# RMSNorms of a two-layer trunk cut into drawn pieces, with their sums of squares mostly on GpSimd

## The chip, the cores and the metric

The kernel runs on one core of a Trainium2 chip. The metric is device time of one execution in microseconds (us). The engines are named as in the profile: PE is TensorE's matmul row and PEld its weight loads, DVE is VectorE, ACT is ScalarE, POOL is GpSimd, SP the engine whose queue issues nearly all DMAs.

## The reference

1152 tokens (1024 latent, 128 context) of width 1024 pass two layers. Layer 0 mixes by attention and a state-space scan, and ends in an output projection `w_out`; layer 1 mixes by pooling windows of 2, 4, 8 and 16 tokens. Each layer then has an MLP of 4096 hidden units with a squared ReLU. Before each mixer, before each MLP and at the end stands an RMSNorm:

```python
def rmsnorm(x, g):
    xf = x.astype(jnp.float32)
    y = xf * lax.rsqrt(jnp.mean(xf * xf, axis=-1, keepdims=True) + EPS)
    return y.astype(x.dtype) * g

def modulate(h, shift, scale):
    return h * (1 + scale) + shift

def sq_relu_mlp(h, w1, w2):
    return jnp.square(jax.nn.relu(h @ w1)) @ w2
```

So every norm needs, for each token, the sum of 1024 squares and one reciprocal root. Five norms are computed; the change touches four of them: norm 1 (after the projection, for MLP 0), norm 2 (after MLP 0, for the pooling), norm 3 (after the pooling, for MLP 1) and the final one (after MLP 1).

## The kernel before, in words

Channels lie on the 128 partitions, tokens along the free dimension. The tokens are three blocks of 384 (NB = 3, BN = 384), the channels eight slices (KT = 8), so one block of the residual is `x[b]`, 128 x 8 x 384 in float32. Block 2 holds 256 latent and 128 context tokens, which have their own gains, so its instructions are often two (SEGS). Matmuls run on a high and a low part of each operand (`hi`, `lo`; three products for one), which is why a weight tile has names such as `wh` and `wl`.

Each norm of a block has four parts:

- **The split** (`gains`, line 303): for each slice ACT writes `hi` = x times gain and DVE writes `lo` = x times gain minus `hi`. Both are the tiles `blk`, of two pools with three buffers each.
- **The sum** (`norm_sums`, line 260): ACT squares slice 0 into the tile `s`, then each later slice into a tile `r` (two buffers), and DVE adds it: seven `TENSOR_TENSOR s<-s,r` for a block. Then one matmul with `selbc` spreads the mean over the partitions, into the PSUM tile `npb`.
- **The root** (`norm_root`, line 279): ACT's Ln and Exp, then four DVE instructions, into the tile `y`.
- The use of `y`: in an MLP it multiplies the first product (`r<-p,y`), in the pooling it is turned by a small matmul `py` into `yc`, at the end it scales the output. `npb` and `py` share one PSUM tag with two buffers.

The stages around the change:

- **Projection** (loop over `order`, lines 1375 to 1396): 24 products of 24 matmuls, the last six being slices 6 and 7 of block 0, then 1, then 2. DVE adds each product to `x[b]`, and meanwhile computes modulation vectors from `mod_v` (`mod_vec`, line 1299: two 128 x 1024 `mj` instructions per vector).
- **MLP** (`mlp`, line 1399): 16 passes over the hidden units; in each, for each block, two first products of 24 matmuls (`p1`, two PSUM buffers), ReLU and square into `ph`, `pl`, and then `second` (line 1404), eight products of 6 matmuls for the block before, each added to `x[b]` (`x<-p,modc,x`).
- **Pooling** (lines 1506 to 1580): ten windows of 128 tokens. `window_products(i+1)` is written before `window_means(i)`; its results `yt` get a shift added on POOL.
- **Final norm** (`final`, line 1583): for blocks 0 and 1 ACT applies the gain and POOL multiplies by `y`; for block 2 DVE does both in one instruction. Each slice is stored by a DMA.

Who draws what: `norm_block` (line 1340) writes a whole norm at once, `norm_pieces` (line 1350) is a generator that yields twice or more, with the whole sum as one piece. At the projection, blocks 0 and 1 use the generator and block 2 the block form; all is then exhausted ahead of MLP 0. After MLP 0 blocks 0 and 1 use the block form, block 2 the generator. In the pooling, blocks 0 and 1 of norm 3 start after windows 3 and 6, two pieces per window.

The order of text isn't the order of an engine's queue. A scheduler runs over all instructions with a cost model, takes among those it holds ready the one that stands first in the text, and fixes each engine's queue; buffers of a tag go in the order of text. At run time each queue is in order. All instructions are made by one wrapper, so nearly all rows say L86; they are told apart by their tiles.

Of the kernel before, what the change touches and what calls it, by code (L numbers as in the profile page):

```python
# [8 lines left out]
F32 = mybir.dt.float32  # L9
# [9 lines left out]
KT = 8  # L19
TL, TX = 1024, 128  # L20
NTOK = TL + TX
NB = 3
# [50 lines left out]
def build(nc, tc, a, o, probe=None):  # L73
# [46 lines left out]
    def tt(e, out, x, y, op):  # L120
        return e.tensor_tensor(out, x, y, op=op)
# [131 lines left out]
        s = modc[layer][:, (3 * half + 1) * 8:(3 * half + 2) * 8]  # L253
        stt(V, avec[i], s, 1.0, ng[:, i, :, None].to_broadcast([128, KT, 2]), ALU.add, ALU.mult)

    last_bc = [None]
    last_p2 = [None]
    last_ms = [None]

    def norm_sums(xb, sq, s4, done=False):  # L260

        if not done:
            A.activation(s4, xb[0], AF.Square)
            for k in range(1, KT):
                A.activation(sq(k), xb[k], AF.Square)
                tt(V, s4, s4, sq(k, True), ALU.add)
            pb = psn([128, BN], F32, "npb", bufs=GB[0], tag="g")
            last_bc[0] = T.matmul(pb, selbc, s4, start=True, stop=True)
            return pb
        ps = psn([128, BN], F32, "nps", bufs=GB[0], tag="g")  # L270
        for k in range(KT):
            g = k % 4
            T.matmul(ps[32 * g:32 * g + 32], ones32, sq(k, True), start=k < 4, stop=k >= 4, tile_position=(0, 32 * g))
        A.activation(s4, ps, AF.Copy)
        pb = psn([128, BN], F32, "npb", bufs=GB[0], tag="g")
        last_bc[0] = T.matmul(pb, selbc, s4, start=True, stop=True)
        return pb

    def norm_root(pb, y, u):
# [5 lines left out]
        V.tensor_scalar(u, u, -0.5, 1.5, op0=ALU.mult, op1=ALU.add)  # L285
        tt(V, y, y, u, ALU.mult)
        return y

    def sq_tile(more=False):
        last = []  # L290

        def sq(k, again=False):
            if not again:
                last[:] = [hid([128, BN], F32, ("ph", "pl")[k % 2]) if more else HP([128, BN], F32, "r", bufs=2)]
            return last[0]

        return sq

    def norm_stats(xb, more=False):
        pb = norm_sums(xb, sq_tile(more), HP([128, BN], F32, "s", bufs=2))  # L300
        return norm_root(pb, HP([128, BN], F32, "y", bufs=YB[0]), HP([128, BN], F32, "s", bufs=2))

    def gains(i, b, k0, xs, hi, lo):

# [72 lines left out]
                A.activation(sqs[b][:, k], xs[b][k], AF.Square)  # L377

    def sums(b):
        return norm_sums(xs[b], lambda k, again=False: sqs[b][:, k], scratch(), True)  # L380

    def root(b, pb):
        ys.append(norm_root(pb, H([128, BN], F32, f"y{b}"), scratch()))
# [953 lines left out]

    rr = [None] * NB

    def norm_block(i, b):  # L1340


        hi, lo = blk2()
        gains(i, b, 0, parts(x[b]), parts(hi), parts(lo))
        if b == 0:
            shift_columns(modc[i // 2][:, 24 * (i % 2):24 * (i % 2) + 8], hi, lo)
        rr[b] = norm_stats(parts(x[b]))
        return hi, lo

    def norm_pieces(i, b, out, first):  # L1350

        hi, lo = blk2()
        out.append((hi, lo))
        y = rr[b] = HP([128, BN], F32, "y", bufs=YB[0])

        def split_(k):
            gains(i, b, k, *(parts(t[:, k:k + 2]) for t in (x[b], hi, lo)))
            if b == 0 and k == KT - 2:
                shift_columns(modc[i // 2][:, 24 * (i % 2):24 * (i % 2) + 8], hi, lo)

        if first:
            for k in range(0, KT, 2):
                split_(k)
            yield
        pb = norm_sums(parts(x[b]), sq_tile(), HP([128, BN], F32, "s", bufs=2))
        yield
        norm_root(pb, y, HP([128, BN], F32, "s", bufs=2))
        if not first:
            for k in range(0, KT, 2):
                yield  # L1370
                split_(k)

    h1, nps = [], []
    wo = {}
    order = [(d, b) for d in range(6) for b in range(NB)] + [(d, b) for b in range(NB) for d in range(6, KT)]
    t0, t1 = MODV[0]
    for n, (d, b) in enumerate(order):
        if n == 3:
            kinds()
        for t in range(t0 + 4 * (n - 4) // 3, min(t0 + 4 * (n - 3) // 3, t1)) if n >= 4 else ():  # L1380
            mod_vec(0, t)
            if t == t1 - 1:
                mod_bias(0, t0, t1)
                scale_vec(1)
        for dd in range(d, min(d + 2, KT)):
            if dd not in wo:
                wo[dd] = weights(a["w_out"][dd], [128, KT, 128], nm="w2", nb=3, pool=W2)
        p = p2([128, BN])
        mm_cat(p, wo[d], b)
        add_to(b, d, p, modc[0][:, 16:24])  # L1390
        if d == KT - 1 and b < NB - 1:
            nps.append(norm_pieces(1, b, h1, GF[b]))
        elif d == KT - 1:
            h1.append(norm_block(1, b))
        if nps and next(nps[0], 0) == 0:
            nps.pop(0)


    def mlp(layer, h, after, extra=None):
        gate = modc[layer][:, 40:48]  # L1400
        prev = None
        y = list(rr)

        def second(w2, b, hd_):
            for d in range(KT):
                p = p2([128, BN])
                n = 0
                for j in range(2):
                    for wi, hi_ in ((0, 0), (0, 1), (1, 0)):
                        T.matmul(p, w2[j][wi][:, d], hd_[j][hi_], start=n == 0, stop=n == 5)  # L1410
                        n += 1
                add_to(b, d, p, gate)

        for c in range(NFF // 2):
            w1 = [weights(a["w1"][layer, 2 * c + j], [128, KT, 128]) for j in range(2)]
            w2 = []
            for j in range(2):
                raw = raw_tile([128, KT, 128])
                dma(raw, a["w2"][layer, 2 * c + j].rearrange("p (k m) -> p k m", k=KT))
                hi = W2([128, KT, 128], F32R, "w2h", bufs=3)  # L1420
                lo = W2([128, KT, 128], F32R, "w2l", bufs=3)
                A.activation(hi, raw, AF.Copy)
                tt(V, lo, raw, hi, ALU.subtract)
                w2.append((hi, lo))
            cf = []
            for b in range(NB):
                hh = []
                for j in range(2):
                    n = BX if b == 0 else BN
                    p = p1([128, BX])  # L1430
                    mm3(p[:, :n], w1[j], [parts(t[:, :, :n]) for t in h[b]], KT)
                    if b == 0:
                        cf.append(HP([128, 2], F32, "cf", bufs=6))
                        V.tensor_copy(cf[j], p[:, BN:BX])
                    r = HP([128, BN], F32, "r", bufs=2)
                    tt(V, r, p[:, :BN], y[b], ALU.mult)
                    for s0, s1, q in SEGS[b]:
                        A.activation(r[:, s0:s1], r[:, s0:s1], AF.Relu, bias=cf[j][:, q:q + 1])
                    ph = hid([128, BN], F32R, "ph")
                    A.activation(ph, r, AF.Square)  # L1440
                    s = HP([128, BN], F32, "s", bufs=2)
                    tt(V, s, r, r, ALU.mult)
                    pl = hid([128, BN], F32R, "pl")
                    tt(V, pl, s, ph, ALU.subtract)
                    hh.append((ph, pl))
                if extra is not None:
                    extra(c, b)
                if prev is not None:
                    second(*prev)
                    if c == NFF // 2 - 1 and b > 0:  # L1450
                        after(b - 1)
                prev = (w2, b, hh)
        second(*prev)
        after(NB - 1)

    hs = []

    def after_mlp0(b):
        if b == 0:
            scale_vec(2)  # L1460
            scale_vec(3)
            tt(V, gps, modc[1][:, 16:24], pscale[:, :, None].to_broadcast([128, KT, 2]), ALU.mult)
        if b < 2:
            hs.append(norm_block(2, b))
        else:
            nps.append(norm_pieces(2, 2, hs, True))
            next(nps[0])

    def mods_1(c, b):
        if c < 12:  # L1470
# [2 lines left out]
            if c == 11 and b == 2:  # L1473
                mod_bias(1, 0, 48)

    for g in nps:
        for _ in g:
            pass
    nps.clear()
    mlp(0, h1, after_mlp0, mods_1)  # L1480


# [23 lines left out]
    def window_products(i):  # L1506
        s0 = 112 * i if i < 9 else TL
        b, e = divmod(s0, BN)
        if i in (0, SH1):
            csh[i > 0] = shift_products(int(i > 0))  # L1510
        if e + 128 <= BN:
# [60 lines left out]
    for i in range(10):  # L1572
        if i < 9:
            ws.append(window_products(i + 1))
        window_means(i, ws[i])
        if i in (3, 6, 9):
            nps.append(norm_pieces(3, i // 3 - 1, h2, i == 9))
        for _ in range(NP if 0 < i < 9 else 20 if i else NQ):
            if nps and next(nps[0], 0) == 0:
                nps.pop(0)  # L1580


    def final(b):
        y = norm_stats(parts(x[b]), b > 0)
        for k in range(KT):
            xk = x[b][:, k]
            if k not in FP[b]:
# [1 line left out]
            else:  # L1589
                A.activation(xk, xk, AF.Copy, scale=ng[:, 4, k:k + 1])  # L1590
                tt(P, xk, xk, y, ALU.mult)
            dma(o["y"][b][:, k], xk)

    mlp(1, h2, final)
    tc_ln.__exit__(None, None, None)
    W2.close()
    WA[0].close()
# [135 lines left out]
```

## Time and profile before

| what | value |
|---|---|
| three runs | 2549.8, 2550.6, 2551.59 us (median 2550.6) |
| the profiled execution | 2552.76 us |
| its span in the trace | 2551.0 us |
| mean granted clock of TensorE | 0.969 of 2.4 GHz |
| PE, PEld, DVE busy | 94%, 90%, 70% of the span |
| ACT, POOL busy | 34%, 10% of the span |

Read it from the top: the run's time is 1.8 us over the span; PE is busy in all but some 150 us, part of which lies in the first 700 us, which the change leaves alone but for a reordered buffer. A busy PE can still be slow, when the granted clock is at the lower of its two levels (1.2 and 2.4 GHz; 0.5 and 1.0 in the profile). The later part is: projection up to about 797 us, MLP 0 to 1629, pooling to 1713, MLP 1 to 2528, and what follows.

### The profile page before, as it was taken

What the parts mean: (1) busy time and instruction counts of PE and PEld (TensorE: products, weight loads), DVE (VectorE), ACT (ScalarE), POOL (GpSimd) and SP (SyncE); (2) the same over time, 40 slices, a digit from 0 to 9 for tenths busy, and PEclk for the clock granted to TensorE, in tenths of its full rate; (3) what the DMA queues carried; (4) which work ended last, traced back from release to release, by engine and by line L of the source; (5) the groups of instructions that cost most, each with busy time, mean ns of one, the idle gap of its engine ahead of it and who ended that gap; (6) DMA issues with size and microseconds to landing.
All of it is one profiled execution on the core that took longest, in us unless ns stands there. A gap on an engine that the chain in (4) does not pass through costs nothing.

```text
span 2551.0 us, 36404 instructions
## 1 busy us (share of the span) xinstructions
PE 2399.8 (94%) x14070; PEld 2296.1 (90%) x14070; DVE 1792.0 (70%) x3583; ACT 877.2 (34%) x1663; POOL 267.0 (10%) x274
## 2 busy tenths in 40 slices
PE   7987898898997999999999999889999999999996
PEld 3876697787897999999999999879999999999996
DVE  7379865889788777767777655886565555555557
ACT  4453365777615221222222222562122222222214
POOL 5455612100000000000000000120000000000002
PEclk8998998999998999999999999989999999999998
DMA  6334688423353232322332110011111111111102
GB/s 244 82 104 126 192 200 229 105 57 81 129 191 108 67 91 68 98 75 75 91 91 79 50 34 25 1 50 50 42 50 34 50 34 50 34 50 42 42 9 74
DMA packets 106491, 210.86 MB, mean 83 GB/s; under 512 B 10576, under 2 KB 67664, under 8 KB 105936
## 3 DMA queue, kind: packets, MB, share of 16 engines
q1 hardware_dynamic: 104080, 203.01, 27.0%
q10 hardware_dynamic: 2240, 5.54, 0.6%
q8 instruction: 111, 1.82, 0.3%
q14 instruction: 60, 0.49, 0.1%
HBM read 176.95 MB, written 31.56 MB: 82 GB/s over the span
## 4 chain that ended last, share of the span: by engine, by line
PE 64%; DVE 11%; issue 5%; ACT 4%; DMA 4%; POOL 1%; SPq 0%; POOLq 0%; DVEq 0%; ACTq 0%
PE p L86 61%; DVE mj L86 2%; DVE blk L86 1%; DMA raw<-in_w_dram 1%; DVE sc L86 1%; DMA raw<-in_mod_v_dram 1%; PE SP L86 1%; DVE nm L86 1%; ACT e L86 1%; PE tp L86 1%; DVE x L86 1%; DVE s L86 1%; ACT blk L86 1%; DVE zz L86 1%; DVE w2l L86 1%
## 5 line engine op out<-in xcount | busy, mean ns | idle before, releaser
L86 PE MATMUL p<-blk,wh 128*128 128x384 f32 (+1 forms) x3072 | 794.2, 340 | 0.0
L86 DVE SCALAR_TENSOR_TENSOR x<-p,modc,x 128x384 f32<-128x384 f32 (+2 forms) x1056 | 513.6, 513 | 142.6 <-PE p L86 138.7
L86 PEld LDWEIGHTS p<-blk,wh 128*128 128x128 f32 x3072 | 561.5, 189 | 1.6 <-issue 1.2
L86 PE MATMUL p<-blk,wl 128*128 128x384 f32 (+1 forms) x1536 | 520.8, 339 | 0.0
L86 PE MATMUL p<-ph,w2h 128*128 128x384 f32 x1536 | 514.9, 335 | 3.7 <-DVE x L86 3.7
L86 PE MATMUL p<-pl,w2h 128*128 128x384 f32 x1536 | 513.9, 335 | 0.0
L86 PE MATMUL p<-ph,w2l 128*128 128x384 f32 x1536 | 513.6, 334 | 0.0
L86 ACT ACTIVATE r<-r,cf 128x384 f32<-128x384 f32 (+2 forms) x256 | 129.8, 531 | 691.6 <-DVE r L86 691.5
L86 PEld LDWEIGHTS p<-ph,w2h 128*128 128x128 f32 x1536 | 288.3, 188 | 6.2 <-DVE x L86 3.6
L86 PEld LDWEIGHTS p<-blk,wl 128*128 128x128 f32 x1536 | 289.5, 188 | 0.1
L86 PEld LDWEIGHTS p<-pl,w2h 128*128 128x128 f32 x1536 | 288.3, 188 | 0.3
L86 PEld LDWEIGHTS p<-ph,w2l 128*128 128x128 f32 x1536 | 288.3, 188 | 0.1
L86 DVE TENSOR_TENSOR r<-p,y 128x384 f32<-128x384 f32 x192 | 106.2, 554 | 188.9 <-PE p L86 188.7
L86 ACT ACTIVATE wh<-raw 128x1024 fp32r<-128x1024 f32 x80 | 84.7, 1060 | 349.7 <-PE p L86 312.1
L86 DVE SCALAR_TENSOR_TENSOR mj<-raw,cb 128x1024 f32<-128x1024 f32 x128 | 156.1, 1220 | 13.6 <-DMA raw<-in_mod_v_dram 12.6
L86 ACT ACTIVATE w2h<-raw 128x1024 fp32r<-128x1024 f32 x74 | 77.3, 1057 | 221.2 <-PE p L86 161.5
L86 PE MATMUL pmm<-lo,wh 128*128 128x384 f32 (+1 forms) x384 | 137.8, 359 | 7.8 <-DVE lo L86 7.5
L86 PE MATMUL pmm<-hi,wh 128*128 128x384 f32 (+1 forms) x384 | 141.0, 368 | 0.8 <-ACT wh L86 0.8
L86 PE MATMUL pmm<-hi,wl 128*128 128x384 f32 (+1 forms) x384 | 136.6, 356 | 1.2 <-DVE wl L86 1.2
L86 DVE TENSOR_TENSOR s<-r 128x384 f32<-128x384 f32 x192 | 106.5, 555 | 40.1 <-ACT r L86 40.0
L86 POOL TENSOR_TENSOR pl<-pl,mx 128x256 f32<-128x256 f32 x18 | 18.6, 1039 | 1024.1 <-ACT pl L86 1024.1
L86 DVE TENSOR_TENSOR wl<-raw,wh 128x1024 fp32r<-128x1024 f32 x76 | 98.7, 1300 | 22.1 <-ACT wh L86 21.8
(278 smaller groups left out, 3346.5 us busy)
## 6 DMA issues: line engine op xcount, KB each, us to landing
raw<-in_w_dram SPq DMA_DIRECT2D x128, 512.0 KB, 3.6
raw<-in_mod_v_dram SPq DMA_DIRECT2D x64, 512.0 KB, 3.6
raw<-in_mod_w_dram SPq DMA_DIRECT2D x25, 512.0 KB, 4.6
raw<-in_w_in_dram SPq DMA_DIRECT2D x16, 512.0 KB, 4.8
Kd<-kS SPq DMA_DIRECT2D x32, 176.0 KB, 4.8
qS<-zz SPq DMA_DIRECT2D x12, 384.0 KB, 2.7
Q<-qS SPq DMA_DIRECT2D x32, 144.0 KB, 4.7
x<-in_x_dram SPq DMA_DIRECT2D x3, 1536.0 KB, 7.3
```

The costliest lines, as they stand in the source:

```text
L86: ins = f(*args, **kw)
```

## The change

All norms of the four sites become generators in small pieces, and a list `nps` of them is drawn from by `pull`, one piece at a time, between the products of the projection, of the MLPs' `second` and first products, and of the pooling. `until` draws as far as a use needs. The sum is kept in `y` itself (before: `s`), and the adds go to an engine that is passed in: `P` (POOL) for norms 1 and 2 and for blocks 0 and 1 of norm 3, `V` (DVE) for block 2 of norm 3 and for the final norm. In the pooling four pieces are drawn per window in place of two. The norm of the last block after each MLP gets its pieces (`post`) directly behind each add of the last `second`.

```diff
+    def pull():
+        if nps and next(nps[0], 0) == 0:
+            nps.pop(0)
+    def until(what, i, b):
+        while (i, b) not in what:
+            pull()
+    def begin(g):
+        next(g)
+        nps.append(g)
+    def summer(b, acc, e):
+        def square(k):
+            if k == 0:
+                A.activation(acc, x[b][:, k], AF.Square)
+            else:
+                sq = HP([128, BN], F32, "r", bufs=2)
+                A.activation(sq, x[b][:, k], AF.Square)
+                tt(e, acc, acc, sq, ALU.add)
+        def means():
+            pb = psn([128, BN], F32, "npb", bufs=GB[0], tag="g")
+            T.matmul(pb, selbc, acc, start=True, stop=True)
+            return pb
...
+    def norm_gen(i, b, out, order, e):
         hi, lo = blk2()
         out.append((hi, lo))
         y = rr[b] = HP([128, BN], F32, "y", bufs=YB[0])
+        square, means = summer(b, y, e)
...
+        if order == "both":
+            for k in range(KT):
+                square(k)
+                if k % 2:
+                    split_(k - 1)
+                yield
+        if order == "split":
+            for k in range(0, KT, 2):
+                split_(k)
+                yield
+        if order != "both":
+            for k in range(0, KT, 2):
+                square(k)
+                square(k + 1)
+                yield
+        yield
+        pb = means()
+        yield
+        norm_root(pb, y, HP([128, BN], F32, "s", bufs=2))
+        rooted.add((i, b))
+        if order == "sums":
             for k in range(0, KT, 2):
                 yield
                 split_(k)
...
-        if d == KT - 1 and b < NB - 1:
-            nps.append(norm_pieces(1, b, h1, GF[b]))
-        elif d == KT - 1:
-            h1.append(norm_block(1, b))
-        if nps and next(nps[0], 0) == 0:
-            nps.pop(0)
+        if d == KT - 1:
+            begin(norm_gen(1, b, h1, "split", P))
+        else:
+            pull()
...
                 add_to(b, d, p, gate)
+                if post:
+                    next(post)
+                pull()
...
+                    if c == 0:
+                        until(halved, 2 * layer + 1, b)
                     p = p1([128, BX])
                     mm3(p[:, :n], w1[j], [parts(t[:, :, :n]) for t in h[b]], KT)
...
+                    if c == 0:
+                        until(rooted, 2 * layer + 1, b)
                     r = HP([128, BN], F32, "r", bufs=2)
...
-        second(*prev)
-        after(NB - 1)
+        last = after(NB - 1)
+        second(*prev, last)
+        nps.append(last)
...
         if b < 2:
-            hs.append(norm_block(2, b))
+            begin(norm_gen(2, b, hs, "split", P))
         else:
-            nps.append(norm_pieces(2, 2, hs, True))
-            next(nps[0])
+            return norm_gen(2, b, hs, "both", P)
...
-    for g in nps:
-        for _ in g:
-            pass
-    nps.clear()
     mlp(0, h1, after_mlp0, mods_1)
...
         if i in (3, 6, 9):
-            nps.append(norm_pieces(3, i // 3 - 1, h2, i == 9))
-        for _ in range(NP if 0 < i < 9 else 20 if i else NQ):
-            if nps and next(nps[0], 0) == 0:
-                nps.pop(0)
+            begin(norm_gen(3, i // 3 - 1, h2, "split" if i == 9 else "sums", V if i == 9 else P))
+        for _ in range(4 if i else 0):
+            pull()
...
+    def final_gen(b):
+        y = HP([128, BN], F32, "y", bufs=YB[0])
+        square, means = summer(b, y, V)
+        for k in range(KT):
+            square(k)
+            yield
+        yield
+        pb = means()
+        yield
+        norm_root(pb, y, HP([128, BN], F32, "s", bufs=2))
         for k in range(KT):
...
             dma(o["y"][b][:, k], xk)
+            yield
...
     mlp(1, h2, final)
+    while nps:
+        pull()
```

Nothing else of the arithmetic or of the DMAs changes: the same squares, 84 adds, 12 spreading matmuls and 24 stores are issued.

## Rows read from the trace of the kernel before

**Rows 1.** The page: span, and busy time of each engine.

```profile
span 2551.0 us, 36404 instructions
PE 2399.8 (94%) x14070; PEld 2296.1 (90%) x14070; DVE 1792.0 (70%) x3583; ACT 877.2 (34%) x1663; POOL 267.0 (10%) x274
```

**Rows 2.** Windows: stretch, its length, busy us of each engine, clock, DMA.

```profile
core 0: us, PE busy (x) PEld busy (x) DVE busy (x) ACT busy (x) POOL busy (x), PEclk, DMA share, GB/s
780.00:805.50 25.50, 24.32 (x137) 23.71 (x135) 25.24 (x57) 16.40 (x37) 0.00 (x0) 1.00 0.21 63
805.50:827.00 21.50, 8.21 (x29) 6.34 (x28) 18.09 (x36) 10.07 (x20) 0.00 (x0) 0.68 0.29 98
1596.00:1629.50 33.50, 31.97 (x181) 30.57 (x179) 30.49 (x66) 22.09 (x49) 0.00 (x0) 1.00 0.00 1
1629.50:1644.00 14.50, 8.33 (x44) 7.67 (x43) 14.48 (x38) 7.79 (x20) 3.91 (x1) 0.65 0.00 1
1671.80:1685.00 13.20, 8.64 (x34) 7.34 (x34) 11.92 (x27) 6.18 (x15) 3.41 (x4) 0.61 0.01 1
1696.30:1709.00 12.70, 7.91 (x31) 6.53 (x31) 11.00 (x25) 7.38 (x17) 3.07 (x3) 0.60 0.01 2
1721.60:1730.00 8.40, 3.82 (x12) 3.14 (x12) 6.77 (x13) 5.87 (x11) 0.00 (x0) 0.80 0.49 131
2528.20:2551.00 22.80, 1.65 (x2) 0.50 (x2) 16.21 (x25) 2.38 (x5) 9.99 (x8) 0.57 0.39 138
```

**Rows 3.** Timeline of PE: start, us, instruction, idle before and releaser.

```profile
786.68 0.91 PE L86 MATMUL npb<-s,selbc 128*128 128x384 f32 x2 [1.18 <-DVE s L86]
...
810.69 1.27 PE L86 MATMUL npb<-s,selbc 128*128 128x384 f32 x2 [4.89 <-DVE s L86]
820.35 1.65 PE L86 MATMUL npb<-s,selbc 128*128 128x384 f32 x2 [8.39 <-DVE s L86]
...
1639.10 0.58 PE L86 MATMUL p<-w2l,blk 128*128 128x256 f32 x1 [4.34 <-DVE w2l L86]
...
1675.75 1.65 PE L86 MATMUL npb<-s,selbc 128*128 128x384 f32 x2 [3.92 <-DVE s L86]
...
1726.26 1.65 PE L86 MATMUL npb<-s,selbc 128*128 128x384 f32 x2 [4.58 <-DVE s L86]
```

**Rows 4.** Groups of DVE's instructions from 780 to 822 us: count, busy, mean ns.

```profile
L86 DVE SCALAR_TENSOR_TENSOR blk<-x,avec,blk 128x384 fp32r<-128x384 f32 (+2 forms) x32 | 14.2, 514 | 0.0
L86 DVE SCALAR_TENSOR_TENSOR mj<-raw,cb 128x1024 f32<-128x1024 f32 x7 | 8.5, 1221 | 0.1
L86 DVE TENSOR_TENSOR s<-s,r 128x384 f32<-128x384 f32 x15 | 8.3, 554 | 0.7 <-ACT r L86 0.4
```

**Rows 5.** Timeline of ACT during the last-but-four product of the projection.

```profile
775.67 0.52 ACT L86 ACTIVATE r<-x 128x384 f32<-128x384 f32 x1 [1.96 <-DVE x L86]
```

**Rows 6.** Timeline of POOL from 2505 to 2545 us.

```profile
2508.38 9.06 POOL L86 TENSOR_TENSOR x<-x,y 128x384 f32<-128x384 f32 x8 [795.98 <-DVE y L86]
2530.22 9.99 POOL L86 TENSOR_TENSOR x<-x,y 128x384 f32<-128x384 f32 x8 [12.77 <-ACT ph L86]
```

**Rows 7.** Timeline of DVE from 2509 us to the end.

```profile
2513.26 0.61 DVE L86 SCALAR_TENSOR_TENSOR x<-p,modc,x 128x384 f32<-128x384 f32 x1
...
2530.84 1.23 DVE L86 TENSOR_TENSOR s<-s,ph 128x384 f32<-128x384 f32 x1
...
2537.24 1.16 DVE L86 TENSOR_TENSOR s<-s,pl 128x384 f32<-128x384 f32 x1
...
2543.68 4.32 DVE L86 SCALAR_TENSOR_TENSOR x<-x,pack,y 128x384 f32<-128x384 f32 x8
```

**Rows 8.** Timeline of DVE: first and last of seven sums, norm 3, block 0.

```profile
1669.32 0.55 DVE L86 TENSOR_TENSOR s<-s,r 128x384 f32<-128x384 f32 x1
...
1675.13 0.56 DVE L86 TENSOR_TENSOR s<-s,r 128x384 f32<-128x384 f32 x1
```

**Rows 9.** Timeline of PE: first matmuls of two successive windows' means.

```profile
1665.30 0.59 PE L86 MATMUL p<-mx,ph 128*128 128x112 f32 x4
...
1669.89 0.59 PE L86 MATMUL p<-mx,ph 128*128 128x112 f32 x4
```

More of the change, by code (lines that the diff above doesn't have):

```diff
@@ L254, in scale_vec, with norm_sums @@
         stt(V, avec[i], s, 1.0, ng[:, i, :, None].to_broadcast([128, KT, 2]), ALU.add, ALU.mult)
-    last_bc = [None]
     last_p2 = [None]
     last_ms = [None]
[L260 to L269, printed above, removed]
+    def norm_sums(sq):
         ps = psn([128, BN], F32, "nps", bufs=GB[0], tag="g")
@@ L272, in norm_sums @@
             g = k % 4
-            T.matmul(ps[32 * g:32 * g + 32], ones32, sq(k, True), start=k < 4, stop=k >= 4, tile_position=(0, 32 * g))
+            T.matmul(ps[32 * g:32 * g + 32], ones32, sq[:, k], start=k < 4, stop=k >= 4, tile_position=(0, 32 * g))
+        s4 = scratch()
         A.activation(s4, ps, AF.Copy)
         pb = psn([128, BN], F32, "npb", bufs=GB[0], tag="g")
-        last_bc[0] = T.matmul(pb, selbc, s4, start=True, stop=True)
+        T.matmul(pb, selbc, s4, start=True, stop=True)
         return pb
@@ L287, in norm_root @@
         return y
[L289 to L301, printed above, removed]
     def gains(i, b, k0, xs, hi, lo):
@@ L379, in sums @@
     def sums(b):
-        return norm_sums(xs[b], lambda k, again=False: sqs[b][:, k], scratch(), True)
+        return norm_sums(sqs[b])
     def root(b, pb):
@@ L1338, in build @@
     rr = [None] * NB
[L1340 to L1350, printed above, removed]
+    h1, nps, rooted, halved = [], [], set(), set()
+    def pull():
[19 more added lines that the diff above has]
+            return pb
+        return square, means
+    def norm_gen(i, b, out, order, e):
         hi, lo = blk2()
@@ L1359, in split_ @@
                 shift_columns(modc[i // 2][:, 24 * (i % 2):24 * (i % 2) + 8], hi, lo)
-        if first:
+            if k == KT - 2:
+                halved.add((i, b))
+        if order == "both":
[5 more added lines that the diff above has]
+        if order == "split":
             for k in range(0, KT, 2):
                 split_(k)
-            yield
-        pb = norm_sums(parts(x[b]), sq_tile(), HP([128, BN], F32, "s", bufs=2))
+                yield
[6 more added lines that the diff above has]
+        pb = means()
         yield
         norm_root(pb, y, HP([128, BN], F32, "s", bufs=2))
-        if not first:
+        rooted.add((i, b))
+        if order == "sums":
             for k in range(0, KT, 2):
@@ L1371, in norm_pieces @@
                 split_(k)
-    h1, nps = [], []
     wo = {}
@@ L1402, in mlp, with second @@
         y = list(rr)
-        def second(w2, b, hd_):
+        def second(w2, b, hd_, post=None):
             for d in range(KT):
@@ L1508, in window_products @@
         b, e = divmod(s0, BN)
+        until(rooted, 2, b)
+        if e + 128 > BN:
+            until(rooted, 2, b + 1)
         if i in (0, SH1):
@@ L1576, in build @@
         if i in (3, 6, 9):
-            nps.append(norm_pieces(3, i // 3 - 1, h2, i == 9))
-        for _ in range(NP if 0 < i < 9 else 20 if i else NQ):
-            if nps and next(nps[0], 0) == 0:
-                nps.pop(0)
-    def final(b):
-        y = norm_stats(parts(x[b]), b > 0)
+            begin(norm_gen(3, i // 3 - 1, h2, "split" if i == 9 else "sums", V if i == 9 else P))
[11 more added lines that the diff above has]
+        norm_root(pb, y, HP([128, BN], F32, "s", bufs=2))
         for k in range(KT):
@@ L1592, in final @@
             dma(o["y"][b][:, k], xk)
+            yield
+    def final(b):
+        if b < 2:
+            begin(final_gen(b))
+        else:
+            return final_gen(b)
     mlp(1, h2, final)
+    while nps:
+        pull()
     tc_ln.__exit__(None, None, None)
```

## The prediction

> **What bounds the kernel now.** Read the page's busy times first: PE has 2399.8 of 2551.0 us [rows 1], so a change that adds no speed to matmuls can win only where PE stands still or runs at the lower clock. The windows come next, to find those places in the part that the change touches [rows 2]; for each I count as lost its length less PE's busy time times the granted clock (an estimate, since busy matmuls overlap). Projection to MLP 0: 25.50 - 24.32 = 1.2, and 21.50 - 8.21 x 0.68 = 15.9, together 17.1 us. End of MLP 0 and first window: 33.50 - 31.97 = 1.5, and 14.50 - 8.33 x 0.65 = 9.1, together 10.6. Pooling, block 0 of norm 3: 13.20 - 8.64 x 0.61 = 7.9. Block 1: 12.70 - 7.91 x 0.60 = 8.0. Block 2, at the start of MLP 1: 8.40 - 3.82 x 0.80 = 5.3. That is 48.9 us, and behind the last product stand 22.8 us in which PE does next to nothing.
>
> The timeline of PE then tells what it waits for [rows 3]: five of the six waits, of 1 to 8 us, are at `npb`, released by DVE's tile `s`, the sum of squares, and one is for a pool weight `w2l` that DVE made late (block 1 of norm 3 looks like block 0). PE is in order, so a waiting `npb` holds back products that have all they need. DVE is why the sum is late: from 780 to 805.5 it is busy 25.24 of 25.50 us, and from 1629.5 to 1644 14.48 of 14.50 [rows 2]. In the 42 us from 780 its largest groups are 32 splits (14.2 us), 7 `mj` (8.5 us) and 15 sums (8.3 us) [rows 4].
>
> **The change, part by part.**
>
> *What is moved.* The sums of norms 1 and 2 (21 adds each) and of two blocks of norm 3 (14) go to POOL: 56 adds at 0.55 us [rows 4], 31 us off DVE, of which only what lay in the full stretches counts. No POOL sum exists before. The nearest row is POOL's 128x384 product of two SBUF tiles: 9.06 and 9.99 us for eight, 1.13 to 1.25 each [rows 6]. I take 1.25, the row with DVE at work on like operands: 8.75 us for a block's seven against 7 x 0.55 = 3.9 on a free DVE. Squares, splits, roots, matmuls and DMAs keep their number, so they cost nothing extra; POOL issues no DMA here, and its own work in the pooling (three shift adds a window) is what the sums can hold up. SP's queue sees the same loads, and the same 24 stores as before.
>
> *What the move costs DVE.* While POOL multiplied at 2530, DVE's own sums took 1.23 us, not 0.55 [rows 7, 4]: 0.68 us more each. An add from PSUM beside POOL at 2513 took 0.61, no more than elsewhere [rows 7, 6]. So a POOL add is free beside work from PSUM and costs DVE up to 0.68 us beside a split, an `mj` or a weight split. Bounds: 0 to 0.68; I take half, 0.34, since DVE's work in these stretches is of both kinds, against 0.55 saved. The Trainium skill (Perfetto Trace Analysis, Optimizing Scalar/DVE Operations) warns that moving work between GpSimd and VectorE "might not help", as they share a read port, and SBUF — State Buffer (Who interferes with whom) says that a VectorE instruction with two SBUF inputs is blocked by a GpSimd one that reads SBUF. The 1.23 and 0.61 agree; by that rule at its full price 56 adds would give back 38 us for the 31 saved.
>
> *Projection to MLP 0 (17.1 lost).* DVE saves 21 x (0.55 - 0.34) = 4 us, which alone wouldn't fill the gap. The order does more: before, all of norm 1 stood ahead of MLP 0, and `r<-p,y` of block 0, which frees the first PSUM buffers, shared its two `r` buffers with squares of blocks 1 and 2. Now only block 0's sum stands ahead of it, and PE has four first products and eight second ones to run before it needs block 2's root. POOL has time: block 0's early slices are squared from 775.67 on [rows 5], so 21 x 1.25 = 26 us end near 803 to 807, before PE comes to block 2. The `mj` there serve layer 1 and can wait. I leave 4.6 us: three waits of about 1.2, as at 786.68 [rows 3], and 1 for DVE. Gain 12.5; bounds 4 (a chain that PE still waits for) and 17.1.
>
> *End of MLP 0 (10.6 lost).* The wait ends with `w2l`, behind block 2's splits, and the drawn order keeps those splits ahead of it. The 14 sums of blocks 0 and 1 come off (7.7 us), 21 POOL adds put back 7.1 at half price, 14.3 at full. Net -0.6; I take a gain of 1, bounds -6.6 (a loss) and 10.6.
>
> *Pooling, blocks 0 and 1 (7.9 and 8.0 lost).* Before, the sum takes 1669.32 to 1675.69, 6.4 us [rows 8]; on POOL 8.75, so it ends 2.35 later. But `means` is now written a window later, behind `py` of that window with which it shares buffers, and a window is 4.6 us (1665.30 to 1669.89) [rows 9]. Gain 4.6 - 2.35 = 2.25 each, 4.5 in all. Bounds: -4.7 (the later order changes nothing) and 15.9. POOL's shift adds queue between the sums; what would be late next is `window_means`.
>
> *Block 2 of norm 3 (5.3 lost).* The sum stays on DVE but is drawn behind the first products of MLP 1, of which PE has four and eight second ones before it needs this root: gain 5.3, the whole loss; bound below 0.
>
> *The tail (22.8).* Before, block 2's sums ran beside POOL's scaling of block 1 until 2538.40, the scalings of block 2 began 5.3 us later and took 4.32, and the span ended 3.0 us after them [rows 7]. Now each square follows its add, so the sum should end near 2531 (last product 2528.2, then some 3 us for the add, the square and the sum). With the same 5.3, scaling starts at 2536.3. POOL is busy until 2540.2 [rows 6]; at 1.25 each three scalings fit in until then, five more at 0.54 end at 2542.8, plus 3.0 gives 2545.8, a gain of 5.2. Bounds 1.7 (all eight at 1.25) and 7.4 (all free). I take 5. Drawing block 1's final pieces behind block 2's could delay POOL; that is inside the bounds.
>
> *Sum:* 12.5 + 1 + 4.5 + 5.3 + 5 = 28.3 us. The profiled execution took 2552.76, 1.8 over its span, and the median of the runs is 2.2 below it: 2552.8 - 28.3 - 2.2 = 2522.3, so **2522 us**.
>
> **The rivals.**
>
> *PE waits for POOL's chains (slower).* A chain of seven takes 8.75 us against 3.9 on a free DVE, 4.9 us more, on eight blocks. Where the scheduler's model holds POOL cheaper than it is, it puts `npb` too early in PE's queue, and everything behind waits. At the full price of eight chains that is 39 us against the 24 that the other parts give (without the pooling's 4.5): 15 slower, 2566. It decides from five exposed chains of eight. For it: `npb` already is where PE waits, and DVE's port conflict lengthens both sides. Against it: PE's drawn order leaves products between. The skill's rule on the shared port, cited above, would bring this about. Chance 0.14.
>
> *Part of it only.* POOL and DVE block each other enough that the projection's gap closes halfway (6), MLP 0's end and the pooling give nothing, block 2 of norm 3 its 5.3, the tail 2.4: 13.7, 2537. For it: full DVE in just these stretches. Chance 0.25.
>
> *Nearly all of it.* 17.1, then 6, 10, 5.3 and 8: 46, 2504. It needs POOL's adds mostly beside PSUM work. Chance 0.15.
>
> *The change doesn't do what it says.* The scheduler hoists work by itself, as the square at 775.67 shows, ahead of the block's last product [rows 5], so new order in the text may leave PE's queue as it was: within 5 us, 2550.6. Against it: buffers and `npb` against `py` do follow the text. Chance 0.08.
>
> **How the numbers follow.** The forecast has 0.38, with a range of its own of 2512 to 2532. About 0.2% (5 us) is what a measurement can tell from no change. Faster is 0.38 + 0.25 + 0.15 = 0.78, the same 0.08, slower 0.14. The range runs from 2500 (a little under the fourth case) to 2549: it leaves out the slow rival and about half of the last, some 0.18.
>
> **What would show each step.** POOL should have 56 instructions `y<-y,r` near 1.2 us, DVE 28 of them near 0.55 and no `s<-s,r` in these stages. PE's windows from 797 to 830 should be full at clock 1.0 but for waits of about 1 us; the wait at `w2l` near 1639 should remain, shorter or not by some us; those at `npb` in the pooling should halve, and the one at 1726 be gone. Splits and weight splits on DVE should show some at 1 to 1.8 us beside POOL. PE's last product should end some 23 us earlier, with 17 to 18 us behind it. The forecast is wrong if PE waits for POOL's `y` for more than 2 us at several `npb`, or if DVE stays full in both stretches and PE's gap there is as long as it was.

## The result: slower by 0.75%, and the profile after

| kernel | median us | runs | span of the profiled run |
|---|---|---|---|
| before | 2550.2 | 2548.3 to 2551.59 | 2551.0 |
| changed | 2570.3 | 2564.88 to 2571.11 | 2568.4 |

The ratio is 1.0075, 95% interval 1.0057 to 1.0092: some 20 us slower, where I forecast 28 faster. The time lies 21 us above the range, and even beyond the slow rival's 2566.

First the changed kernel's page (span, busy times), to be held against [rows 1]:

```profile
span 2568.4 us, 36440 instructions
PE 2409.5 (94%) x14070; PEld 2305.2 (90%) x14070; DVE 1786.0 (70%) x3527; ACT 879.1 (34%) x1663; POOL 329.8 (13%) x330
```

POOL gained 62.8 us of work and 56 instructions, as the change says. DVE lost 56 instructions, but its busy time fell by 6.0 us only, since others became longer (how much is worked out under K2 below). Next PE's list of waits (what was awaited, us in all, how often, the longest):

```profile
PE npb L86 <- POOL y L86: 15.3, 5, 4.2
PE npb L86 <- DVE y L86: 11.5, 1, 11.5
PE p L86 <- DVE wl L86: 6.7, 1, 6.7
PE p L86 <- DVE w2l L86: 6.1, 1, 6.1
PE p L86 <- DVE r L86: 5.1, 1, 5.1
```

The prediction named as its own refutation "waits for POOL's `y` for more than 2 us at several `npb`". There are five, of 15.3 us: 4.16 and 3.83 at the start of MLP 0, 2.25 in its last pass, 2.61 and 2.50 in the pooling. The `w2l` wait at the end of MLP 0 is longer than the 4.34 of [rows 3]; a wait for `wl` is new; and the `npb` of the tail, which waited before as well (10.3 us), waits 11.5.

To see where the time went I cut the spans at PE's products of known tiles (first and last of the projection, last of MLP 0, first and last of the windows' means, last of MLP 1). Times are differences of those landmarks; the kernels in the four columns on the right are those of the experiments below.

| stage, us | before | changed | K1: sums on DVE | K2: short chains | K3: K1, final norms whole | K4: K3, norm 3 late |
|---|---|---|---|---|---|---|
| projection | 105.0 | 103.0 | 103.0 | 103.0 | 103.0 | 102.9 |
| to end of MLP 0 | 832.7 | 833.8 | 818.5 | 824.3 | 820.5 | 819.7 |
| to the first means | 17.5 | 21.7 | 19.1 | 19.5 | 19.5 | 18.9 |
| means, first to last | 66.0 | 65.2 | 58.6 | 54.7 | 59.4 | 58.8 |
| to end of MLP 1 | 814.9 | 817.4 | 815.8 | 816.6 | 818.2 | 812.8 |
| tail | 23.2 | 34.2 | 34.2 | 34.5 | 19.7 | 19.6 |

The start of the projection, which no edit touches, lies between 686.4 and 693.1 us in these runs, so two spans can differ by up to 6.7 us for nothing; stages are the safer reading, and medians of several runs the verdict. Against before the changed kernel loses 4.2 us at the end of MLP 0, 2.5 up to the end of MLP 1 and 11.0 in the tail, and where I expected most, 12.5 at the start of MLP 0, it loses 1.1.

**At the start of MLP 0.** POOL's timeline (start, us, instruction, idle before and releaser) of the changed kernel:

```profile
785.99 1.14 POOL L86 TENSOR_TENSOR y<-y,r 128x384 f32<-128x384 f32 x1 [5.47 <-ACT r L86]
813.14 10.12 POOL L86 TENSOR_TENSOR y<-y,r 128x384 f32<-128x384 f32 x7 [26.01 <-ACT r L86]
831.53 7.74 POOL L86 TENSOR_TENSOR y<-y,r 128x384 f32<-128x384 f32 x7 [8.28 <-ACT r L86]
```

ACT's timeline beside the first of the two chains:

```profile
810.70 1.12 ACT L86 ACTIVATE r<-r,cf 128x384 f32<-128x384 f32 x2 [4.35 <-DVE r L86]
812.55 0.92 ACT L86 ACTIVATE r<-x 128x384 f32<-128x384 f32 x2
814.25 0.53 ACT L86 ACTIVATE r<-x 128x384 f32<-128x384 f32 x1 [0.77 <-POOL y L86]
816.19 0.53 ACT L86 ACTIVATE r<-x 128x384 f32<-128x384 f32 x1 [1.42 <-POOL y L86]
```

And what PE does behind them:

```profile
810.81 0.98 PE L86 MATMUL p<-blk,wh 128*128 128x384 f32 x2 [5.09 <-DVE r L86]
...
823.31 1.65 PE L86 MATMUL npb<-y,selbc 128*128 128x384 f32 x2 [4.16 <-POOL y L86]
...
839.32 1.21 PE L86 MATMUL npb<-y,selbc 128*128 128x384 f32 x2 [3.83 <-POOL y L86]
```

POOL stands idle for 26 us after block 0's last add. Blocks 1 and 2 are squared into `r`, and the MLP's own `r<-p,y` takes the same two buffers. They go in the order of text, and the drawn text puts block 1's squares behind block 0's first products. So ACT can square block 1 only at 812.55, after the ReLU (`r<-r,cf`) of block 0; the two buffers then come back one POOL add at a time (releaser POOL `y`), and PE meets `npb` while the chain runs.

**What DVE pays meanwhile.** DVE's timeline of the same moment, with POOL adding from 813.14 to 823.26:

```profile
813.27 2.03 DVE L86 SCALAR_TENSOR_TENSOR mj<-raw,cb 128x1024 f32<-128x1024 f32 x1
...
815.22 2.02 DVE L86 TENSOR_TENSOR w2l<-raw,w2h 128x1024 fp32r<-128x1024 f32 x1
```

An `mj` takes 1.22 us in [rows 4]. POOL's adds lose as well; the first row is an add beside an `mj`, the second one behind it, when DVE does nothing (819.20 to 826.16):

```profile
814.29 1.87 POOL L86 TENSOR_TENSOR y<-y,r 128x384 f32<-128x384 f32 x1
...
820.12 0.99 POOL L86 TENSOR_TENSOR y<-y,r 128x384 f32<-128x384 f32 x1
```

Three adds of this chain took 1.85 to 1.88 us, so some 2.6 of its 10.1 us are this conflict.

**In the tail** PE's one wait, then POOL's and DVE's timelines:

```profile
2545.99 2.92 PE L86 MATMUL npb<-y,selbc 128*128 128x384 f32 x4 [11.50 <-DVE y L86]
```

```profile
2529.84 9.35 POOL L86 TENSOR_TENSOR x<-x,y 128x384 f32<-128x384 f32 x8 [813.54 <-DVE y L86]
2551.52 9.65 POOL L86 TENSOR_TENSOR x<-x,y 128x384 f32<-128x384 f32 x8 [12.33 <-issue]
```

```profile
2533.50 1.35 DVE L86 TENSOR_TENSOR y<-y,r 128x384 f32<-128x384 f32 x1
...
2541.99 2.55 DVE L86 TENSOR_TENSOR y<-y,r 128x384 f32<-128x384 f32 x4 [0.45 <-ACT r L86]
...
2554.03 8.61 DVE L86 SCALAR_TENSOR_TENSOR x<-x,pack,y 128x384 f32<-128x384 f32 x8
```

Everything has slid one block back. Block 0's scaling, on POOL from 2508.38 in [rows 6], now runs from 2529.84, beside block 2's sums on DVE; block 1's sums end behind the last product, its `npb` stands next to block 2's (the x4 above), and its scaling on POOL stands beside block 2's on DVE, which takes 8.61 us in place of 4.32 [rows 7].

### The profile page after: what moved, and what is told of

Read it like the earlier page. It is cut to its first block, busy times and chain, and to the rows that moved or that the text cites. A ratio compares the mean times of both kernels' runs of the same rounds, so it can differ in the third digit from the quotient of the medians.

```text
span 2568.4 us, 36440 instructions
## 1 busy us (share of the span) xinstructions
PE 2409.5 (94%) x14070; PEld 2305.2 (90%) x14070; DVE 1786.0 (70%) x3527; ACT 879.1 (34%) x1663; POOL 329.8 (13%) x330
## 4 chain that ended last, share of the span: by engine, by line
PE 65%; DVE 10%; issue 5%; ACT 4%; DMA 4%; POOL 2%; SPq 0%; DVEq 0%; ACTq 0%; POOLq 0%
PE p L86 61%; POOL y L86 2%; DVE mj L86 2%; DMA raw<-in_w_dram 1%; DVE x L86 1%; PE SP L86 1%; DVE nm L86 1%; ACT e L86 1%; PE tp L86 1%; DVE sc L86 1%; DVE blk L86 1%; DMA raw<-in_mod_v_dram 1%; PE pmm L86 1%; DVE zz L86 1%; DVE e L86 1%
## 5 line engine op out<-in xcount | busy, mean ns | idle before, releaser
L86 POOL TENSOR_TENSOR y<-y,r 128x384 f32<-128x384 f32 x56 | 67.8, 1216 | 962.5 <-ACT r L86 959.6
L86 DVE SCALAR_TENSOR_TENSOR mj<-raw,cb 128x1024 f32<-128x1024 f32 x128 | 159.4, 1246 | 12.7 <-DMA raw<-in_mod_v_dram 11.5
L86 POOL TENSOR_TENSOR x<-x,y 128x384 f32<-128x384 f32 x16 | 19.0, 1221 | 825.9 <-DVE y L86 813.5
```

What stands on the lines that cost most here:

```text
L86: ins = f(*args, **kw)
```

## The experiments

Two theories stood after this reading. **P**: the sums on POOL make them late, the drawn order itself is sound. **O**: the drawn order makes things late, whichever engine adds.

**K1, the sums back on DVE**, with every drawn piece left where the change put it:

```diff
-            begin(norm_gen(1, b, h1, "split", P))
+            begin(norm_gen(1, b, h1, "split", V))
...
-            begin(norm_gen(2, b, hs, "split", P))
+            begin(norm_gen(2, b, hs, "split", V))
...
-            return norm_gen(2, b, hs, "both", P)
+            return norm_gen(2, b, hs, "both", V)
...
-... V if i == 9 else P))
+... V))
```

> The changed kernel with the 56 sums of norms 1 to 3 back on VectorE, drawn order kept. Theory P (GpSimd's slow chains and the shared port cost the time): the five waits at npb for POOL's y, 15.3 us together, shrink to a few us, w2l and wl come earlier, and the time falls by 10 to 18 us to 2552 to 2560. Theory O (the drawn order costs it: squares share the two r buffers with the MLP's r in the order of the text, and the final pieces of block 1 stand behind those of block 2): the sums of blocks 1 and 2 of norm 1 still start only after the ReLU of the block before (about 812 and 831 us), the tail keeps its 33.8 us, and the time falls by at most 5 us, to 2565 to 2570.

Measured: 2540.7 us (2537.38 to 2544.28), ratio 0.9965 [0.9952, 0.9978]. That is 28 to 30 us under the changed kernel. O alone falls as the cause in these stages, and P had its price too low. With the same order of text the stage up to the end of MLP 0 is 818.5, 14.2 under before: PE's timeline in place of the first two of the three waits above (there is none at block 2's `npb` either):

```profile
801.67 0.59 PE L86 MATMUL p<-blk,wh 128*128 128x384 f32 x2 [2.03 <-DVE r L86]
811.92 0.48 PE L86 MATMUL npb<-y,selbc 128*128 128x384 f32 x1
```

Against the changed kernel that stage is 15.3 us shorter. Of the five waits for POOL (15.3 us too, by coincidence) 10.2 lie in it; the wait for `r` is 3.1 shorter (5.09 against 2.03). The rest goes with the lower clock, as an estimate: from 810.8 to 815.8 us, behind the longer wait, the changed kernel's granted clock is 0.50, and K1's is 1.00 in the 5 us behind its own.

The tail stays at 34.2: that loss isn't POOL's sums.

**The final norms of blocks 0 and 1 whole**, once on the changed kernel (sums on POOL), once on K1 (this is K3 in the table):

```diff
         if b < 2:
-            begin(final_gen(b))
+            for _ in final_gen(b):
+                pass
```

> The changed kernel with the final norms of blocks 0 and 1 written whole again at the end of their products, and only block 2's pieces drawn. Theory O: block 0's scaling on POOL starts near 2515 again, block 1's sum ends before the last product, the tail shrinks from 33.8 us to 17 to 23, so 2555 to 2561 in all. Theory P, for the tail: POOL's scaling blocks VectorE's sums whatever the order, so the tail stays above 28 us and the time above 2564.

> Both edits: sums on VectorE, and the final norms of blocks 0 and 1 written whole. If the two causes are independent, the gains of the two runs add: theory P expects 2537 to 2548 (10 to 18 and 10 to 14), theory O 2551 to 2558 (up to 5 and 10 to 14).

Measured: 2554.1 (2550.97 to 2557.64), 1.0018 [1.0009, 1.0027], tail 19.6, just under O's 2555; and K3 2529.7 (2526.14 to 2536.36), 0.9922 [0.9903, 0.994], tail 19.7, faster than either theory had it, since K1 had already been so. So drawing these two norms costs 16 us on one base and 11 on the other, by the medians; 14.5 by the tails of the profiled runs. Here O is right. K3's rows, PE, then POOL and DVE:

```profile
2514.97 1.65 PE L86 MATMUL npb<-y,selbc 128*128 128x384 f32 x2 [6.87 <-DVE y L86]
```

```profile
2506.51 9.25 POOL L86 TENSOR_TENSOR x<-x,y 128x384 f32<-128x384 f32 x8 [9.90 <-issue]
```

```profile
2520.05 4.32 DVE L86 SCALAR_TENSOR_TENSOR x<-x,pack,y 128x384 f32<-128x384 f32 x8
```

POOL is done with block 1 at 2515.76, before block 2's scaling starts, and that takes 4.32 again.

**Which block of the two?** K3 with one of them drawn again (`if b == 0: begin(final_gen(b))`, then the same for `b == 1`):

> Base: sums on VectorE, final norms whole (2529.7). Here only block 0's final norm is drawn in pieces again, block 1's stays whole. If the late scaling of block 0 on POOL (which then runs beside block 2's sums) is what cost 15 us in the tail: 2537 to 2543. If it is block 1's pieces behind block 2's: 2528 to 2533.

> Same base, only block 1's final norm drawn in pieces, block 0's whole. If block 1's pieces behind block 2's are the cost (its sum, npb and root end after the last product, its scaling on POOL then slows VectorE's scaling of block 2 from 0.54 to 1.08 us each): 2538 to 2546, the tail 29 us or more. If block 0's late scaling is: 2528 to 2533.

Measured: 2535.6 (2533.77 to 2537.15), 0.9943 [0.9927, 0.996], and 2536.5 (2532.71 to 2537.11), 0.9943 [0.9929, 0.9958]: 5.8 and 6.8 us over K3. Each lies between the two ranges expected of it, so both blocks seem to pay, about half each; but the intervals overlap K3's, and the traces are the better witness. In the first, block 0's scaling moved to 2502.51, beside block 1's root and block 2's first sums, and block 1's to 2512.47 to 2521.71, beside the rest of block 2's sums. The tail stays (20.0), and the loss lies ahead of it: MLP 1 takes 823.1 us in place of 818.2, and PE waits in its last products for DVE's late add to `x`:

```profile
2511.52 0.66 PE L86 MATMUL p<-ph,w2h 128*128 128x384 f32 x1 [3.30 <-DVE x L86]
```

In the second the tail grows, from 19.7 to 27.6: block 1's scaling stands beside block 2's, which takes 8.62 again.

**Is it the place of POOL's chains, or their length?** First the place: the changed kernel with norm 1 exhausted ahead of MLP 0, sums still on POOL:

```diff
+    while nps:
+        pull()
     mlp(0, h1, after_mlp0, mods_1)
```

> The changed kernel with all pieces of norm 1 drawn out ahead of MLP 0, as before, their sums still on POOL. Theory O: the squares of blocks 1 and 2 then stand ahead of the MLP's r in the order of the buffers, POOL adds without a pause from about 786 us, block 2's npb comes by 815 and the third gap (833 to 839) is gone; but the first r of the MLP waits for the last square, so the gap after the first two products stays: no gain or up to 5 us, the two late waits at npb merged into one. Theory P: POOL's 14 adds one after the other take 17 us from the last projection product, PE stands still from 805 to 818 or later, and the time is the same or up to 5 us longer.

Measured: 2560.0 (2557.41 to 2562.24), 1.0036 [1.0023, 1.0048], some 10 us less than the changed kernel; to the end of MLP 0 828.3, 5.5 less. Neither theory had this as its likely outcome. POOL's timeline shows why:

```profile
775.15 1.02 POOL L86 TENSOR_TENSOR y<-y,r 128x384 f32<-128x384 f32 x1 [9.22 <-ACT r L86]
781.71 9.63 POOL L86 TENSOR_TENSOR y<-y,r 128x384 f32<-128x384 f32 x7 [5.54 <-ACT r L86]
793.17 8.16 POOL L86 TENSOR_TENSOR y<-y,r 128x384 f32<-128x384 f32 x6 [1.83 <-ACT r L86]
806.48 2.07 POOL L86 TENSOR_TENSOR y<-y,r 128x384 f32<-128x384 f32 x2 [5.15 <-ACT r L86]
```

With all of norm 1 ahead POOL works through from 781.71, and PE waits once, 7.35 us at 808.60. So on POOL the drawn place is worse than the old one by 5.5 us in this stage, while on DVE it seems the better one (before against K1, 14.2; K1 with norm 1 ahead wasn't run). This run also shows that a chain on POOL needn't cost: the stage is 4.4 us shorter than before's 832.7. Before, with DVE full, block 2's `npb` came 23 us behind the last projection product (820.35 in [rows 3]), here 15.

Then the shared `r`: norm 1's squares put into `ph` and `pl`, the hidden units' tiles, in place of `r`.

```diff
-                sq = HP([128, BN], F32, "r", bufs=2)
+                sq = hid([128, BN], F32, ("ph", "pl")[k % 2]) if own else HP([128, BN], F32, "r", bufs=2)
```

> The changed kernel, sums on POOL, but norm 1's squares in the four-buffer tiles ph and pl and no longer in the two r buffers that the MLP's ReLU uses. From the last projection product to MLP 0's last product the kernel before takes 832.7 us, the changed one 833.8, the one with sums on VectorE 818.5. Theory B (POOL's slow chain is only exposed because the squares queue behind the MLP's r): block 1's adds start by 795 us and not at 812, the wait of 4.2 us at its npb goes, and the stage falls to 820 to 826, the whole to 2556 to 2563. Theory L (a chain of 8 to 10 us on POOL is too long wherever it starts): the stage stays at 830 or more and the whole within 4 us of 2570.

Measured: 2567.8 (2565.98 to 2570.77), 1.007 [1.0055, 1.0085]: no gain that can be told. It doesn't decide: the MLP's `ph` and `pl` go in the order of text too, and block 1's first add here still came at 808.84. Tiles of the squares' own would decide it; that wasn't tried. The run before this one, where the chains did start early, speaks for a part of B.

**K2, the length alone.** The changed kernel with all 56 POOL adds, of which only the first three of a block feed `y`; the other four double their own square in place. The mean so lacks squares 4 to 7; POOL and DVE have as many instructions as in the changed kernel.

```diff
-                tt(e, acc, acc, sq, ALU.add)
+                d = sq if e is P and k > 3 else acc
+                tt(e, d, d, sq, ALU.add)
```

> The changed kernel with its 56 POOL adds, but only the first three of each block's seven feed the spreading matmul; the other four double their own square in place, so the mean lacks squares 4 to 7. POOL and DVE have the same number of instructions on the same kinds of tiles; only the chain ahead of npb is shorter, some 4 to 6 us less per block. If PE waits for the length of POOL's chains, the stage from projection to the last product of MLP 0 falls from 833.8 toward the 818 to 822 of the kernels with the sums on DVE, and the time to 2548 to 2560. If it is DVE, slowed by POOL beside it, that makes the products late, the stage stays at 829 or over and the time at 2563 to 2571.

Measured: 2543.9 (2540.48 to 2544.7), 0.9975 [0.9966, 0.9985]: 26 us less than the changed kernel, below what the length theory expected, and some 3 us over K1, where the intervals overlap. The stage up to the end of MLP 0 came to 824.3, a little over the theory's 818 to 822 and under the rival's 829. POOL is nearly as full as it was (61.8 us for the two kinds, against 67.8):

```profile
806.66 4.97 POOL L86 TENSOR_TENSOR y<-y,r 128x384 f32<-128x384 f32 x3 [27.27 <-ACT r L86]
811.60 4.16 POOL L86 TENSOR_TENSOR r<-r 128x384 f32<-128x384 f32 x4
```

DVE is slowed by it as it was (an `mj`):

```profile
806.79 2.03 DVE L86 SCALAR_TENSOR_TENSOR mj<-raw,cb 128x1024 f32<-128x1024 f32 x1
```

And PE's waits for POOL are gone:

```profile
PE npb L86 <- POOL y L86: 0.8, 2, 0.4
```

So most of what the sums cost on POOL is the length of the chain that `npb` waits for. What POOL costs DVE is read from the same instructions in the two kernels, the splits first (changed, then K1):

```profile
L86 DVE SCALAR_TENSOR_TENSOR blk<-x,avec,blk 128x384 fp32r<-128x384 f32 (+1 forms) x96 | 54.2, 615 | 1.7 <-ACT blk L86 1.4
...
L86 DVE SCALAR_TENSOR_TENSOR blk<-x,avec,blk 128x384 fp32r<-128x384 f32 (+1 forms) x96 | 44.7, 518 | 0.0
```

By means times counts the splits take 9.3 us longer, `w2l` 3.2 and `mj` 3.0, 15.5 in all; in K2 the three take 13 longer. The busy times agree roughly: without the 56 adds K1's 1792.9 would be 1767.0 (neighbouring instructions overlap, so an add counts less than 0.55), and the changed kernel has 1786.0, 19 more, K2 1780.4, 13 more. So K2 keeps most of DVE's loss and still gains 26 us. This doesn't give that loss a price of its own: K2 also spares DVE the adds, a part of the chain's length is the conflict itself, as shown above, and the scheduler placed each `npb` anew in each kernel. Up to the end of MLP 0 5.8 us over K1 remain; 3.3 of it is the wait for `r` (5.32 against 2.03), behind block 0's root. In all three kernels the root stands on ACT behind a weight split `w2h` that waits for its load; ACT comes to the root 6.1 us behind the last projection product in K1, 9.0 in the changed kernel and 9.3 in K2. Why the load is later there wasn't settled.

**K4, block 2 of norm 3 later.** In K3, DVE made 16 splits of that block ahead of MLP 1's first `wl`, for which PE waited 4.78 us (6.65 in the changed kernel). K4 draws them behind:

```diff
-        for _ in range(4 if i else 0):
+        for _ in range(4 if 0 < i < 9 else 0):
             pull()
```

> Same base, but the pieces of block 2 of norm 3 behind the first are drawn only in MLP 1, after its first weights are written, not four of them after the last window. If the wait of 4.8 us at the weight part wl comes from these splits standing ahead of it in VectorE's queue: it goes, with the slow clock after it, and the time falls by 4 to 7 us to 2523 to 2526. If the weight is late for another reason (its load or its buffer): within 2 us of 2529.7.

Measured: 2526.1 (2522.07 to 2527.25), 0.9903 [0.9888, 0.9918], against 2529.7 for K3: 3.6 by the medians, where the intervals overlap, and 5.4 in the stage. The wait at `wl` is 0.80 in place of 4.78. The long row of splits is broken up and `wl` comes between them:

```profile
1690.62 1.40 DVE L86 SCALAR_TENSOR_TENSOR blk<-x,avec,blk 128x256 fp32r<-128x256 f32 x4
1691.94 1.22 DVE L86 TENSOR_TENSOR wl<-raw,wh 128x1024 fp32r<-128x1024 f32 x1
```

In the changed kernel it was:

```profile
1721.32 5.34 DVE L86 SCALAR_TENSOR_TENSOR blk<-x,avec,blk 128x256 fp32r<-128x256 f32 x16
...
1727.05 1.21 DVE L86 TENSOR_TENSOR wl<-raw,wh 128x1024 fp32r<-128x1024 f32 x1
```

**Block 2's final pieces.** K4 with block 2's final norm whole behind the last product:

```diff
-        second(*prev, last)
+        second(*prev, None if layer else last)
```

> The best kernel so far (sums on DVE, final norms of blocks 0 and 1 whole, block 2 of norm 3 late), with block 2's final norm also written whole behind the last second product, as before, and no longer a piece behind each add. If drawing its squares and adds behind each add is what shortened the tail from 23.2 to 19.6, the tail goes back to 22.5 to 24 and the time rises by 3 to 4 us over 2526. If the scheduler orders these by itself anyway, tail and time stay within 1 us.

Measured: 2524.7 (2523.76 to 2526.29), 0.9905 [0.9888, 0.9921], the same as K4 within the intervals. The tail of the profiled run went from 19.6 to 21.7, 2.1 us of the 3 to 4 expected, and the time shows none of it. K4 and this one are faster than both kernels, by about 1% than the one before and 1.7% than the changed one.

## Why the prediction was wrong, step by step

- **"POOL has time: ... 21 x 1.25 = 26 us end near 803 to 807"** (projection to MLP 0, 12.5 us) is the step that failed. The price was right: 56 adds had a mean of 1.22 us. The place was wrong: I let POOL run from 775.67 on, and worked out beside it that only block 0's sum now stands ahead of MLP 0. The two don't go together, since blocks 1 and 2 must then get `r` buffers behind block 0's `r<-p,y`. With norm 1 exhausted ahead, the chains do end at 808.55, near what I had; as the change orders it they end at 839.27. With the sums on DVE the order does gain, 14.2 us in K1; with them on POOL the stage gave back 15.3.
- **The slow rival** (POOL's chains exposed) was the right mechanism in the MLP 0 and pooling stages, and I gave it only 0.14, though the rows spoke for more: `npb` already was where PE waited [rows 3]. It predicted 4.9 us per exposed chain and that five of them would decide; PE shows five waits of 15.3 us in all, 3.1 each. That its 2566 lies near the measured 2570.3 is luck: it counted block 2 of norm 3 and the tail as gains of 10.3, and they lost 13.5.
- **DVE at half price** (0.34 us for each add) held: 15.5 to 19 us over 56 adds are 0.28 to 0.34 each. The Trainium skill (SBUF — State Buffer, Who interferes with whom) says that a VectorE instruction with two SBUF inputs contends with a GpSimd one that reads SBUF. The 2.03 us of an `mj` against 1.22 agree. But K2 shows that this price was not the main one.
- **End of MLP 0** (gain 1, bounds -6.6 to 10.6): a loss of 4.2, inside the bounds. `w2l` behind the splits stayed the wait, as I wrote, and grew from 4.34 [rows 3] to 6.1. A loss of 1.6 stays with the sums on DVE (K1), where PE waits 7.17 us at `npb`.
- **Pooling, blocks 0 and 1** (gain 4.5): 0.8 on POOL, 7.4 in K1, 11.3 in K2. The two waits at `npb` fell from 3.92 and 4.16 to 2.61 and 2.50; I had them halved. The queue is as I wrote: POOL's shift adds `pl` and `ph` stand behind the sums. But what was late next was not `window_means`: PE waited 1.17 and 1.65 us in the window products, for ACT's `pl`, which stands among squares that wait for POOL's adds.

```profile
1674.60 6.61 POOL L86 TENSOR_TENSOR y<-y,r 128x384 f32<-128x384 f32 x6 [0.50 <-ACT r L86]
1681.16 1.04 POOL L86 TENSOR_TENSOR pl<-pl,mx 128x256 f32<-128x256 f32 x1
```

- **Block 2 of norm 3** (gain 5.3): a loss of 2.5. The wait at `npb` (4.58 at 1726.26) is gone, as I wrote, and one of 6.65 at `wl` came in its place. I costed the sum that moved behind MLP 1's products, not the 16 splits that stayed ahead of them, nor what is queued behind those on DVE: `wl`. Drawn later (K4) the stage gains 2.1 on before.
- **The tail** (gain 5): a loss of 11.0. "Drawing block 1's final pieces behind block 2's could delay POOL; that is inside the bounds" is the step. The bound of 1.7 rested on no row for it; drawing blocks 0 and 1 cost 14.5 in the tail (K1 against K3). My sum held block 0's and 1's scalings where they were and moved only block 2's. With those two left whole the tail is 3.5 shorter than before (K3), near the 5; but drawing block 2's pieces is only 2.1 of that, and none of it shows in the time. What the other 1.4 is wasn't settled; the final squares of blocks 1 and 2 also moved from `ph` and `pl` to `r`, which the list of the change leaves out.

By the medians, with the ratios against before: changed +20; without POOL's sums 28 to 30 less (K1); without the drawn final norms a further 11 (K3); with norm 3's splits behind MLP 1's first weights 4 more (K4). That is 24 us under before, with all adds on DVE. It is near the 28 that I had given to the change as a whole, but the parts differ: up to the end of MLP 0 15.1 (forecast 12.5), to the first means -1.4 (1), pooling 7.2 (4.5), MLP 1 2.1 (5.3), tail 3.6 (5).

## What to carry over

Before moving a reduction to a slower engine, look whether a waiting instruction stands at its end, and when the chain can start: here PE waited 2.3 to 4.2 us at five of eight such places, though the engine was 87% idle. And when work is cut into pieces that are drawn later, follow each buffer tag and each queue in the new order of text, for every block: here two shared buffers kept POOL idle for 26 us. In this kernel drawn pieces paid where only a sum and its `npb` were drawn behind products; they cost where a scaling on POOL or a weight split on DVE came late by them.

## What the runs showed of the hardware

- The cost of POOL beside DVE goes both ways: `mj` and `w2l` of 128x1024 took 2.02 to 2.03 us in place of 1.22, and eight scalings `x<-x,pack,y` 8.61 in place of 4.32; POOL's add took 1.85 to 1.88 beside `mj` and `w2l` and 0.99 while DVE stood idle.
- In sum it was small: 56 adds on POOL made DVE's splits, `w2l` and `mj` 15.5 us longer. K2, where the three are still 13 us longer, is 26 us faster than the changed kernel.
